# Weight tiles and small tiles move to the upper end of SBUF, streamed operands to the lower end

## The chip, the cores and the metric

The kernel runs on 1 core of a Trainium2 chip. The metric is device time in microseconds (us) of one execution. TensorE (PE) multiplies, ScalarE (ACT) and VectorE (DVE) work element by element, GpSimd (POOL) helps them, SyncE (SP) issues most DMAs. A matmul has two operands in SBUF: a block of 128x128 numbers that a weight load (PEld) puts into the array, and an operand of up to 512 columns that is streamed through it. The load of the next matmul runs while the present one streams.

## The reference

Two transformer-like blocks work on 512 tokens of width 1024, in float32:

```python
x = x + 0.5 * swiglu(rms_norm(x, ffn1_norm), ffn1_w_in, ffn1_w_out)       # hidden width 2816
mix = banded and compressed/selected attention of rms_norm(x) @ w_mix_in
x = x + mix @ w_mix_out
x = x + 0.5 * swiglu(rms_norm(x, ffn2_norm), ffn2_w_in, ffn2_w_out)
proj = rms_norm(x) @ w_in                         # gated linear attention and retention, 4 heads each
h = x + (sigmoid(mga) * (o_gla @ w_br_gla) + sigmoid(mgb) * (o_ret @ w_br_ret)) @ w_out
h = h + experts(rms_norm(h))                      # 32 experts, 2 of 8 in one group for each token
out = rms_norm(h)
```

## The kernel before, in words

Activations lie transposed, a tile for each 128 features with the 512 tokens along its columns. For accuracy every large product is made of three: `split` (L84, L85) makes a rounded high part (float32r) and the rest as a low part, and `mm3` issues high x high (L99), the streamed operand's low part (L100), and the weights' low part (L101). `gemm` runs `mm3` over k-tiles, so a product of 8 k-tiles is 24 matmuls of 128x128 against 128x512.

The stages in order of time: the first FFN (to about 381 us), attention (to about 751), the second FFN (to about 1027), the second mixer with gated linear attention (the pool `gla`) and retention (the pool `ret`; to about 1797), the product with `w_out` and the routing (to about 1860), and the experts (to the end).

`load_w` (L87 on) brings 128x1024 weights from HBM into a tile `wraw` (3 buffers), and splits it into `whi` and `wlo` (2 buffers each). What the matmuls stream:

- `xh`, `xl` (8 tiles each, 2 KB of every partition): the scaled input of a stage. Streamed in the products `pg`, `pu` (FFN in) and `pj` (projections). In `vv` they are the loaded block, and `whi`, `wlo` are streamed. The tiles `oh`, `ol` of the last product of mixer 2 take the same places.
- `hh`, `hl` (10 each): the hidden values of an FFN, streamed in its second product `po`.
- `fh`, `fl` (8 each): the heads' outputs in mixer 2, made in `head_out` (L818), streamed in `ya` and `yb`.
- `rh`, `rl`, `sh`, `sl` and others: attention's inner products. In `rs` both operands are `rh` or `rl`.

SBUF is handed out from two ends. Pools of the lower end are stacked upward in the order in which they are opened, those with `side="right"` downward from the upper end. Before, `const`, `wts`, `xhl` and `small` are opened at the lower end and stay, and the pools of the stages follow above them; only the experts' ring of weights (`ring`, L1087) is at the upper end. The ring is opened in `moe_open` and filled by `fill_ring` while the product with `w_out` runs. A pool that takes the place of a released one waits tile by tile for the last reader of what lay there.

The scheduler keeps the written order on PE, ACT and SP. The expert stage's zeroing of three gather rows `xr` (L1095) is POOL's work behind the adds `mt` (L1060), which end mixer 2.

Of the kernel before, what the change touches and what calls it, by code (L numbers as in the profile page):

```python
# [10 lines left out]
F32R = mybir.dt.float32r  # L11
# [28 lines left out]
class Kern:  # L40
    def __init__(self, ctx, tc, A, out, dbg=None, stop=None):
        self.ctx, self.tc, self.nc, self.A, self.out = ctx, tc, tc.nc, A, out
        self.dbg = dbg or {}
        self.stop = stop
        self.sin = None
        e = ctx.enter_context
        self.const = e(tc.tile_pool(name="const", bufs=1))
        self.wp = e(tc.tile_pool(name="wts", bufs=1))
        self.xp = e(tc.tile_pool(name="xhl", bufs=1))
        self.sm = e(tc.tile_pool(name="small", bufs=2))  # L50
        self.dram = e(tc.tile_pool(name="dram", bufs=1, space=bass.MemoryType.DRAM))
        self.ps = e(tc.tile_pool(name="psum", bufs=1, space=PSUM))
        self.xd = self.dram.tile([128, DT, 512], F32, name="xd")
# [732 lines left out]
    def head_out(self, V, c0, nt, sh, sl, wname, w0, gates, wait):  # L786

        nc = self.nc
        vh, vl = V
        O = []  # L790
        ssum = None
        for t in range(nt):
            po = self.ps.tile([128, 512], F32, name="pvo", tag="tp", bufs=2)
            for j in range(4):
                q = slice(128 * j, 512)
                v = slice(c0 + 128 * t, c0 + 128 * t + 128)
                self.mm3(po[:, q], vh[:, j, v], vl[:, j, v], sh[:, j, q], sl[:, j, q], j == 0, j == 3)
            o = self.m2.tile([128, 512], F32, name="o", bufs=4)
            nc.scalar.activation(o, po, AF.Copy)
            sq = self.m2.tile([128, 512], F32, name="osq", bufs=2)  # L800
            nc.scalar.activation(sq, po, AF.Square)
            if ssum is None:
                ssum = sq
            else:
                nc.gpsimd.tensor_tensor(out=ssum, in0=ssum, in1=sq, op=OP.add)
            O.append(o)
        F = self.F

        def rest():
            p = self.ps.tile([128, 512], F32, name="on", tag="pv", bufs=1)  # L810
            nc.tensor.matmul(p, self.ones, ssum, start=True, stop=True)
            r = self.rstd_from(p, 1.0 / (128 * nt), "hr", None)
            for t in range(nt):
                g = gates[t]
                nc.gpsimd.tensor_tensor(out=g, in0=g, in1=r, op=OP.mult)
                o = O[t]
                nc.vector.scalar_tensor_tensor(o, o, self.vcol(wname, w0 + t), g, op0=OP.mult, op1=OP.mult)
                fh = self.m2.tile([128, 512], F32R, name="fh", bufs=8)  # L818
                fl = self.m2.tile([128, 512], F32R, name="fl", bufs=8)
                self.split(o, fh, fl)  # L820
                F.append((fh, fl))
        self.pend = [wait, rest]
        self.flush(0)
# [165 lines left out]
    def mixer2(self):  # L989
        nc, A = self.nc, self.A  # L990
        self.xpool.release()
        self.m2 = self.pool("m2")
        m3 = self.m3 = self.pool("gla")
        self.gmask = m3.tile([128, 8, 128], I32, name="gmask")
        nc.sync.dma_start(self.gmask, A["gmask"])
        ma = self.dram.tile([128, DT, 512], F32, name="ma")
        yb = self.dram.tile([128, DT, 512], F32, name="yb")
        self.pend = None
        self.gla_decay()
        self.F = []  # L1000
        V = None
        for h in range(4):
            if h == 0:
                V = self.vproj(A["wgv"][:, h // 2], False)
            q, k = self.gla_qk(h)
            gates = [self.silu_tile(A["wg"][:, h, 2 + t]) for t in range(2)]
            if h == 2:
                V = self.vproj(A["wgv"][:, h // 2], False)
            self.gla_core(h, q, k, V, gates)
        for n in range(DT):  # L1010
            _, s = self.sigma(self.proj2(A["wma"][:, n]))
            self.flush()
            w = self.load_w(A["wbg"][:, n])
            po = self.acc("ya")
            self.gemm(po, w, self.F, DT)
            t = self.m2.tile([128, 512], F32, name="mt", tag="gate", bufs=4)
            nc.vector.tensor_tensor(out=t, in0=po, in1=s, op=OP.mult)
            nc.sync.dma_start(ma[:, n], t)
        m3.release()
        m3 = self.m3 = self.pool("ret")  # L1020
        self.cs = m3.tile([128, 2, 512], F32, name="csr")
        nc.sync.dma_start(self.cs, self.csd)
        for c in (0, 1):
            nc.vector.tensor_tensor(out=self.cs[:, c], in0=self.cs[:, c], in1=self.rstd, op=OP.mult)
        M = []
        Q = None
        for half in range(2):
            F = self.F = []
            for h in (2 * half, 2 * half + 1):
                Q = Q or self.ret_qk(h, 0)  # L1030
                K = self.ret_qk(h, 1)
                V = self.vproj(A["wrv"][:, h], True)
                gates = [self.silu_tile(A["wr"][:, h, 4 + t]) for t in range(4)]
                self.ret_core(h, Q, K, V, gates)
                Q = None
            if half == 0:
                Q = self.ret_qk(2, 0)
            if half == 1:
                m3.release()
                sp = self.pool("sig")  # L1040
                sg = []
                for n in range(DT):
                    _, g = self.sigma(self.proj2(A["wmb"][:, n]), sp.tile([128, 512], F32, name=f"sg{n}"))
                    sg.append(g)
            self.flush()
            for n in range(DT):
                w = self.load_w(A["wbr"][:, half, n])
                po = self.acc("yb")
                self.gemm(po, w, self.F, DT)
                t = self.m2.tile([128, 512], F32, name="mt", tag="gate", bufs=4)  # L1050
                if not half:
                    nc.scalar.activation(t, po, AF.Copy)
                    nc.sync.dma_start(yb[:, n], t)
                    continue
                nc.sync.dma_start(t, yb[:, n])
                nc.vector.tensor_tensor(out=t, in0=po, in1=t, op=OP.add)
                nc.vector.tensor_tensor(out=t, in0=t, in1=sg[n], op=OP.mult)
                t2 = self.m2.tile([128, 512], F32, name="mt2", tag="vc", bufs=2)
                nc.sync.dma_start(t2, ma[:, n])
                nc.gpsimd.tensor_tensor(out=t, in0=t, in1=t2, op=OP.add)  # L1060
                h = self.xp.tile([128, 512], F32R, name=f"oh{n}", tag=f"xh{n}")
                lo = self.xp.tile([128, 512], F32R, name=f"ol{n}", tag=f"xl{n}")
                self.split(t, h, lo)
                M.append((h, lo))
        sp.release()
        self.m2.release()
        self.moe_open()
        self.open_x()
        self.route_open()
        for n in range(DT):  # L1070
            w = self.load_w(A["wo2"][:, n])
            r = self.old_x(n)
            if n:
                self.fill_ring(2)
            po = self.acc("po2")
            self.gemm(po, w, M, DT)
            nc.vector.tensor_tensor(out=self.x[n], in0=po, in1=r, op=OP.add)
            if n:
                self.route_tile(n - 1)
        self.route_tile(DT - 1)  # L1080
        self.fill_ring(RING + len(EXTRA) - 2 * (DT - 1))
# [700 lines left out]
```

## Time and profile before

| what | us |
|---|---|
| median of 3 runs | 2369.15 (2362.69 to 2371.07) |
| the profiled execution | 2362.63 |
| its span | 2360.8 |
| PE busy in it | 2285.1 (97%) |
| DVE, ACT, POOL busy | 1151.6, 857.0, 401.6 |
| granted TensorE clock, mean | 0.988 of full speed |

PE's records of successive matmuls overlap: the duration of one (some 0.39 us) is longer than the distance from its start to the next start. What a product costs is read from the distance between starts; the duration helps as a second witness.

### The profile page before, as it was taken

The numbers are of one execution on the slowest core, as the hardware profiler recorded it, in microseconds if no ns is written. First come the engines' busy times: TensorE is split into PE (matmuls) and PEld (weight loads), VectorE is DVE, ScalarE is ACT, GpSimd is POOL, SyncE is SP. The second block draws the span as 40 slices with busy tenths as digits, with TensorE's granted clock in tenths as the row PEclk, the third lists the DMA queues.
The fourth block names the chain that finished last, engine by engine and source line by source line (L and its number), as shares of the span: only waits on it lengthen the run. The fifth ranks groups of instructions, "written<-read, shape, count | busy, mean of one in ns | idle before, by whom it ended". The sixth has DMA issues, their size and how long they took to land.

```text
span 2360.8 us, 27739 instructions
## 1 busy us (share of the span) xinstructions
PE 2285.1 (97%) x10344; PEld 1674.6 (71%) x10344; DVE 1151.6 (49%) x2074; ACT 857.0 (36%) x1441; POOL 401.6 (17%) x408
## 2 busy tenths in 40 slices
PE   8999999999999999999999999999999899999997
PEld 6888888777778888878777887787878544444443
DVE  4534444888754343456684445435464333332223
ACT  4322234677642222354454354434553211100002
POOL 1000002435410000014340112203113201111001
PEclk9999999999999999999999999999999899999999
DMA  4533335221143333332213323232337999999997
GB/s 145 187 91 95 100 96 165 81 72 41 46 121 98 90 93 104 108 115 72 64 53 112 108 84 89 84 117 67 90 116 229 352 394 407 406 407 407 404 408 303
DMA packets 126098, 390.83 MB, mean 166 GB/s; under 512 B 15398, under 2 KB 21071, under 8 KB 125704
## 3 DMA queue, kind: packets, MB, share of 16 engines
q1 hardware_dynamic: 121064, 380.10, 47.1%
q10 hardware_dynamic: 2592, 4.72, 0.5%
q0 software_dynamic: 2304, 4.20, 0.5%
q8 instruction: 83, 1.36, 0.2%
q14 instruction: 55, 0.45, 0.1%
HBM read 378.44 MB, written 17.33 MB: 168 GB/s over the span
## 4 chain that ended last, share of the span: by engine, by line
PE 86%; DVE 5%; DMA 3%; ACT 3%; POOL 1%; issue 1%; SPq 0%; POOLq 0%; DVEq 0%; ACTq 0%
PE pg L1326 5%; PE pj L101 5%; PE pj L100 5%; PE pj L99 5%; PE pu L1326 5%; PE po L100 4%; PE po L101 4%; PE po L99 4%; PE pd L1326 4%; PE pu L101 3%; PE pu L99 3%; PE pu L100 3%; PE pg L99 3%; PE pg L101 3%; PE pg L100 3%; PE py L1393 2%
## 5 line engine op out<-in xcount | busy, mean ns | idle before, releaser
L84 ACT ACTIVATE whi<-wraw 128x1024 fp32r<-128x1024 f32 (+2 forms) x290 | 296.1, 1021 | 714.4 <-issue 185.9
L85 DVE TENSOR_TENSOR wlo<-wraw,whi 128x1024 fp32r<-128x1024 f32 (+2 forms) x282 | 347.4, 1232 | 138.2 <-ACT whi L84 128.5
L101 PE MATMUL pj<-xh,wlo 128*128 128x512 f32 x624 | 247.3, 397 | 10.4 <-DVE wlo L85 10.4
L99 PE MATMUL pj<-xh,whi 128*128 128x512 f32 x624 | 250.2, 401 | 0.0
L100 PE MATMUL pj<-xl,whi 128*128 128x512 f32 x624 | 246.3, 395 | 0.0
L157 POOL TENSOR_TENSOR ssq<-ssq,sq 128x512 f32<-128x512 f32 x34 | 52.6, 1547 | 774.1 <-ACT sq L154 772.1
L1326 PE MATMUL pg<-wexp,xs 128*64 128x512 f32 x474 | 164.4, 608 | 2.4 <-DMA wexp<-in_wexp 2.3
L1326 PE MATMUL pu<-wexp,xs 128*64 128x512 f32 x474 | 160.6, 594 | 0.0
L99 PE MATMUL pg<-xh,whi 128*128 128x512 f32 x352 | 138.6, 394 | 8.7 <-ACT xh L142 7.1
L101 PEld LDWEIGHTS pj<-xh,wlo 128*128 128x128 f32 x624 | 118.4, 190 | 36.0 <-DVE wlo L85 12.1
L100 PE MATMUL po<-hl,whi 128*128 128x512 f32 x352 | 139.6, 397 | 0.0
L99 PE MATMUL po<-hh,whi 128*128 128x512 f32 x352 | 139.5, 396 | 0.0
L101 PE MATMUL po<-hh,wlo 128*128 128x512 f32 x352 | 139.5, 396 | 0.0
L100 PE MATMUL pg<-xl,whi 128*128 128x512 f32 x352 | 138.2, 393 | 0.5 <-DVE xl L143 0.5
L101 PE MATMUL pu<-xh,wlo 128*128 128x512 f32 x352 | 137.2, 390 | 0.9 <-DVE wlo L85 0.9
L101 PE MATMUL pg<-xh,wlo 128*128 128x512 f32 x352 | 137.9, 392 | 0.0
L99 PE MATMUL pu<-xh,whi 128*128 128x512 f32 x352 | 137.1, 389 | 0.0
L100 PE MATMUL pu<-xl,whi 128*128 128x512 f32 x352 | 136.9, 389 | 0.0
L99 PEld LDWEIGHTS pj<-xh,whi 128*128 128x128 f32 x624 | 118.6, 190 | 25.7 <-issue 2.6
L100 PEld LDWEIGHTS pj<-xl,whi 128*128 128x128 f32 x624 | 118.2, 189 | 24.7 <-issue 1.7
L1326 PE MATMUL pd<-wexp,hs 128*64 128x512 f32 x484 | 115.7, 599 | 0.0
L1326 PEld LDWEIGHTS pu<-wexp,xs 128*64 128x64 f32 x474 | 49.1, 138 | 78.4 <-issue 77.9
(613 smaller groups left out, 4418.3 us busy)
## 6 DMA issues: line engine op xcount, KB each, us to landing
wexp<-in_wexp SPq DMA_DIRECT2D x358, 512.0 KB
wraw<-in_w1i SPq DMA_DIRECT2D x44, 512.0 KB
wraw<-in_w2i SPq DMA_DIRECT2D x44, 512.0 KB
wraw<-in_wr SPq DMA_DIRECT2D x32, 512.0 KB
wpark<-in_wexp SPq DMA_DIRECT2D x48, 256.0 KB
wraw<-in_wg SPq DMA_DIRECT2D x16, 512.0 KB
wraw<-in_wrv SPq DMA_DIRECT2D x16, 512.0 KB
wraw<-in_wbr SPq DMA_DIRECT2D x16, 512.0 KB
```

The source lines that it names most:

```text
L84: return (self.nc.scalar.activation(hi, src, AF.Copy), (eng or self.nc.vector).tensor_tensor(out=lo, in0=src, in1=hi.bitcast(F32), op=OP.s ...
L85: (eng or self.nc.vector).tensor_tensor(out=lo, in0=src, in1=hi.bitcast(F32), op=OP.subtract))
L99: mm(ps, ah, bh, start=first, stop=False)
L100: mm(ps, ah, bl, start=False, stop=False)
L101: mm(ps, al, bh, start=False, stop=last)
L157: self.nc.gpsimd.tensor_tensor(out=self.ssq, in0=self.ssq, in1=sq, op=OP.add)
L1326: self.pe(self.nc.tensor.matmul(out[r], x[:, r], self.loaded[2 * p + j, c][half], start=first, stop=last))
L1393: self.pe(nc.tensor.matmul(ps, oh[:, i * 128:i * 128 + 128], y[:, hf * 512:hf * 512 + 512], start=(first and j == 0), stop=(j == 1)))
```

## The change

The pools `wts` (weights) and `small` go to the upper end, so `xhl` follows `const` at the lower end and the stages' pools follow `xhl`. A new pool `m2f`, opened before `m2`, holds `fh` and `fl`.

```diff
         self.const = e(tc.tile_pool(name="const", bufs=1))
-        self.wp = e(tc.tile_pool(name="wts", bufs=1))
         self.xp = e(tc.tile_pool(name="xhl", bufs=1))
-        self.sm = e(tc.tile_pool(name="small", bufs=2))
+        self.wp = e(tc.tile_pool(name="wts", bufs=1, side="right"))
+        self.sm = e(tc.tile_pool(name="small", bufs=2, side="right"))
...
-                fh = self.m2.tile([128, 512], F32R, name="fh", bufs=8)
-                fl = self.m2.tile([128, 512], F32R, name="fl", bufs=8)
+                fh = self.m2f.tile([128, 512], F32R, name="fh", bufs=8)
+                fl = self.m2f.tile([128, 512], F32R, name="fl", bufs=8)
...
         self.xpool.release()
+        self.m2f = self.pool("m2f")
         self.m2 = self.pool("m2")
...
         self.m2.release()
+        self.m2f.release()
         self.moe_open()
```

No instruction is added or removed. Where the tiles lie in the two programs as built, in bytes of a partition (first byte of the first and of the last buffer). Every tile starts at a multiple of 32; "even" means a multiple of 64, "odd" 32 more than one.

| tiles | before | | after | |
|---|---|---|---|---|
| `whi`, `wlo` | 30656 to 42944 | even | 212960 to 225248 | odd |
| `xh`, `xl` (`oh`, `ol`) | 47040 to 77760 | even | 18368 to 49088 | even |
| `hh`, `hl` | 121440 to 160352 | odd | 79808 to 118720 | even |
| `fh`, `fl` | 154208 to 184928 | odd | 51136 to 81856 | even |
| `rh`, `rl` | 203360 to 217696 | odd | 161728 to 176064 | even |
| `sh`, `sl`, `vh`, `vl` | 100960 to 133728 | odd | 92096 to 124864 | even |

In time order one thing moves. Of POOL's queue at the end of mixer 2, before (`mt` are mixer 2's last sums, `xr` the rows for the gather, the rest is routing):

```order
L1060 TENSOR_TENSOR mt<-mt,mt_14108 128x512
L1060 TENSOR_TENSOR mt<-mt,mt_14150 128x512
L1060 TENSOR_TENSOR mt<-mt,mt_14192 128x512
L1095 MEMSET xr_14207 128x1024
L1095 MEMSET xr_14208 128x1024
L1095 MEMSET xr_14209 128x1024
L1170 IOTA io 128x64
L1229 IOTA tok 128x4
L1244 IOTA tokens 128x512
```

The same place of POOL's queue after (the lines are two further down in the changed file):

```order
L1061 TENSOR_TENSOR mt<-mt,mt_14111 128x512
L1061 TENSOR_TENSOR mt<-mt,mt_14153 128x512
L1097 MEMSET xr_14211 128x1024
L1097 MEMSET xr_14212 128x1024
L1061 TENSOR_TENSOR mt<-mt,mt_14195 128x512
L1097 MEMSET xr_14213 128x1024
L1172 IOTA io 128x64
L1246 IOTA tokens 128x512
L1231 IOTA tok 128x4
```

Two of the three MEMSETs now stand ahead of the last `mt` sum, and they wait for the end of the last `yb` product, since the rows now lie where `fh` lay. PE, ACT and SP issue the same instructions in the same order; on DVE one small cast of the routing moves by one place.

## Rows read from the trace of the kernel before

**Rows 1.** The page's first part: busy time of each engine and its share of the span.

```profile
PE 2285.1 (97%) x10344; PEld 1674.6 (71%) x10344; DVE 1151.6 (49%) x2074; ACT 857.0 (36%) x1441; POOL 401.6 (17%) x408
```

**Rows 2.** The page's fourth part: shares of the chain of waits that ended last, by engine.

```profile
PE 86%; DVE 5%; DMA 3%; ACT 3%; POOL 1%; issue 1%; SPq 0%; POOLq 0%; DVEq 0%; ACTq 0%
```

**Rows 3.** Windows by stage: the second FFN, mixer 2, the product with `w_out` and the routing, the experts. Columns: window, its length, then busy time and instructions of PE, PEld, DVE, ACT, POOL, the granted clock, the DMA engines' mean share and GB/s.

```profile
752.00:1027.00 275.00, 275.00 (x1198) 224.73 (x1197) 119.65 (x140) 77.71 (x96) 9.82 (x6) 1.00 0.35 104
1027.00:1802.00 775.00, 752.28 (x3440) 614.77 (x3439) 423.30 (x595) 355.89 (x550) 183.07 (x149) 0.98 0.30 91
1802.00:1860.00 58.00, 55.02 (x316) 46.30 (x315) 24.87 (x54) 22.92 (x37) 11.71 (x12) 1.00 0.92 309
1860.00:2343.00 483.00, 472.57 (x2044) 203.77 (x2046) 141.02 (x359) 50.63 (x97) 56.52 (x80) 0.98 1.02 402
```

**Rows 4.** The experts' weights: the issues of their DMAs on SP's queue, count, duration of an issue in ns, first and last start.

```profile
L1101 SPq DMA_DIRECT2D wexp<-in_wexp x358: 327/328/760, 1801.8 to 2331.5; - x179
```

**Rows 5.** Windows on PE alone that hold one kind of product each: `po` (192 matmuls), `pg` and `pu` (336), `pj` between other work (48), `pj` (96), `vv` (96), `yb` (192). Columns as above, of PE alone; the count takes in a record or two that reach over a window's edge.

```profile
105.88:150.86 44.98, 44.98 (x194) 1.00 0.32 94
150.86:227.03 76.17, 76.17 (x338) 1.00 0.32 93
389.25:400.29 11.04, 11.04 (x50) 1.00 0.67 212
1330.84:1352.61 21.77, 21.77 (x98) 1.00 0.33 94
1352.61:1374.37 21.76, 21.76 (x98) 1.00 0.37 111
1752.30:1797.28 44.98, 44.98 (x194) 1.00 0.48 152
```

**Rows 6.** Lines of the views of the tiles `hh`, `xh` and `rh`: instructions, then duration of one in ns (least, median, most), first and last start, and the shapes.

```profile
L99 PEld LDWEIGHTS po<-hh,whi x352: 187/188/192, 105.7 to 1026.0; 128*128 128x128 f32 x176
L99 PE MATMUL po<-hh,whi x352: 392/397/400, 105.9 to 1026.2; 128*128 128x512 f32 x176
...
L99 PE MATMUL pu<-xh,whi x352: 389/389/497, 16.4 to 986.9; 128*128 128x512 f32 x176
...
L99 PE MATMUL vv<-whi,xh x224: 343/389/754, 400.7 to 1670.1; 128*128 128x512 f32 x96, 128*128 128x408 f32 x16
...
L99 PE MATMUL rs<-rh x32: 221/334/390, 1396.1 to 1696.6; 128*128 128x512 f32 x8, 128*128 128x384 f32 x8, 128*128 128x256 f32 x8, 128*128 128x128 f32 x8
```

**Rows 7.** The timeline of PE where a run of `pj` ends and `rs` follows, four places: start, duration (us), line, operands.

```profile
1395.67 0.39 PE L100 MATMUL pj<-xl,whi 128*128 128x512 f32 x1
1395.90 0.40 PE L101 MATMUL pj<-xh,wlo 128*128 128x512 f32 x1
1396.13 0.39 PE L99 MATMUL rs<-rh 128*128 128x512 f32 x1
...
1397.52 0.33 PE L99 MATMUL rs<-rh 128*128 128x384 f32 x1
...
1480.13 0.40 PE L101 MATMUL pj<-xh,wlo 128*128 128x512 f32 x1
1480.37 0.39 PE L99 MATMUL rs<-rh 128*128 128x512 f32 x1
...
1608.24 0.40 PE L101 MATMUL pj<-xh,wlo 128*128 128x512 f32 x1
1608.47 0.39 PE L99 MATMUL rs<-rh 128*128 128x512 f32 x1
...
1692.31 0.40 PE L101 MATMUL pj<-xh,wlo 128*128 128x512 f32 x1
1692.55 0.39 PE L99 MATMUL rs<-rh 128*128 128x512 f32 x1
```

**Rows 8.** PE's groups by line with shapes kept apart: count | busy us, mean ns of one | idle before. L100 and L101 have as many as L99 in each.

```profile
L99 PE MATMUL pj<-xh,whi 128*128 128x512 f32 x624 | 250.2, 401 | 0.0
...
L99 PE MATMUL pg<-xh,whi 128*128 128x512 f32 x352 | 138.6, 394 | 8.7 <-ACT xh L142 7.1 <-ACT rstd_ln L175 1.6
...
L99 PE MATMUL pu<-xh,whi 128*128 128x512 f32 x352 | 137.1, 389 | 0.0
...
L99 PE MATMUL vv<-whi,xh 128*128 128x512 f32 x192 | 75.5, 393 | 0.0
...
L99 PE MATMUL yb<-fh,whi 128*128 128x512 f32 x128 | 51.3, 401 | 0.4 <-ACT fh L84 0.4
...
L99 PE MATMUL ya<-fh,whi 128*128 128x512 f32 x64 | 26.1, 410 | 1.8 <-ACT fh L84 1.8
...
L99 PE MATMUL po<-oh,whi 128*128 128x512 f32 x64 | 25.4, 397 | 0.0
...
L99 PE MATMUL po<-mh,whi 128*128 128x512 f32 x32 | 13.3, 420 | 1.2 <-ACT mh L84 1.2
...
L99 PE MATMUL pvo<-sh,vh 128*128 128x512 f32 x24 | 9.8, 428 | 0.0
```

**Rows 9.** The timelines of PE and of POOL, and the chain of waits, around the end of mixer 2 (start, duration, what).

```profile
1797.04 0.39 PE L101 MATMUL yb<-fh,wlo 128*128 128x512 f32 x1
...
1801.11 2.74 POOL L1095 MEMSET xr<- 128x1024 f32 x3
...
1799.03 2.16 POOL mt L1060
```

## The prediction

> **What bounds the kernel now.** I read the page's busy times and the shares of its chain first: PE is busy 97% of the span, and 86% of the chain that ended last is PE [rows 1, 2]. The windows by stage say where that holds. In the second FFN PE is busy for all of the 275.0 us, in mixer 2 for 752 of 775 [rows 3]. The experts are another case: there the DMA engines are full (mean share 1.02, 402 GB/s) while PE too looks busy [rows 3], because matmuls wait for weights. Their weights are issued from 1801.8 us on [rows 4], behind the weights of the product with `w_out`, whose buffers PE frees. So the kernel is a PE-bound part of about 1800 us, and a DMA-bound tail that begins when the first part is through. A microsecond that PE loses before 1800 us moves the tail and the end with it; one that it loses in the tail is hidden by the transfers. What the change does to the distance between matmuls before 1800 us is the whole question.
>
> That distance has two values for the same instruction (128 columns loaded, 512 streamed, float32r), both at a granted clock of 1.00 [rows 5]. `pg` and `pu`: 76.17 us / 336 = 226.7 ns. `pj`: 21.77 / 96 = 226.8. `vv`, which loads `xh` and streams `whi`: 21.76 / 96 = 226.7. But `po`, which streams `hh`: 44.98 / 192 = 234.3, and `yb`, which streams `fh`: 234.3. The durations part in the same way, 389 against 397 ns, while a weight load takes 188 ns in either and ends long before the next start, so it is not the load that is waited for [rows 6].
>
> What do the slow ones have in common? By the table of places, `pg`, `pu`, `pj` and `vv` stream and load only tiles at even places within the lowest 80 KB. `po` and `yb` stream from odd places above 120 KB and load `whi` from an even one below 43 KB. Two readings are open: the streamed operand's own place costs the 7.5 ns, or the two operands' places not being alike. One kind of spot tells them apart. Where a run of `pj` ends and `rs` follows, the last `pj` streams `xh` from its good place as always, but the load beside it is already `rs`'s block `rh`, odd and high. In all four places this one matmul takes 0.40 us instead of 0.39, and the next start comes 0.23, 0.24, 0.23 and 0.24 us later, 235 ns on average [rows 7]. The stream was as good as before; only the load's place had changed. I take the second reading: unlike places cost about 7.5 ns a matmul. (Whether "unlike" is the odd 32 bytes or the distance I needn't decide, for after the change the weights are both odd and high.)
>
> **The change part by part.** No engine gets or loses an instruction. Each term is a count [rows 6, 8] (a group of L99 times three) times a difference of distances.
>
> 1. `pg`, `pu`, `pj`: 1,056 + 1,056 + 1,872 = 3,984 matmuls stream `xh`/`xl`, even and low. Their weights go from even and low to odd and high. Distance in a run 226.7 -> 234.2, so 7.5 ns. Not all stand in long runs: between other work 48 `pj` took 11.04 us, 230.0 each [rows 5]. I put 400 of the 3,984 there (an estimate) with 4.2 ns. 3,584 x 7.5 + 400 x 4.2 = 26.9 + 1.7 = +28.6 us.
> 2. `vv`: 576 with 512 columns. They stream the weights, now odd and high, and load `xh`, even and low: 576 x 7.5 = +4.3 us.
> 3. `po` from `hh` (1,056), `ya` (192), `yb` (384) and `po` from `mh` (96): the stream becomes even, the weights odd. One kind of unlike pair takes the place of another: 0. If the streamed operand's place were what counts, this is where the change would gain.
> 4. The product with `w_out` streams `oh`/`ol` from `xh`'s places: 192 x 7.5 = 1.4 us. It lies mostly in the third window, where the ring fills and DMA is at 0.92 [rows 3]: between 0 and 1.4, and I take half, +0.7.
> 5. Mixer 2's inner products (`rs`, `pvo`) have both operands odd before and even after. Six `rs` in sequence take 1397.52 - 1396.13 = 1.39 us, 232 each [rows 7]. Of 512 columns there are 24 `rs` [rows 6] and 72 `pvo` [rows 8]. If they fell to 226.7 that would be 96 x 5 = 0.5 us less, and with the narrower ones at most thrice that, 1.5 (an estimate). They run in short stretches, where even good pairs stand at 230 [rows 5]; I take 0 and keep 1.5 for the range.
> 6. POOL: two MEMSETs now precede the last `mt` sum. They wait for the end of the last `yb` product, which starts at 1797.04 and lasts 0.39, and three take 2.74 us [rows 9], two 1.8 to 1.9. So they end at 1799.2 to 1799.3, and the sum, which began at 1799.03 and is on the chain [rows 9], is held up by 0.2 to 0.4 us; behind it `oh` of the last tile and PE's `po` wait. +0.3.
>
> The moved DVE, ACT and DMA operands I cost at nothing: DVE and ACT have 49% and 36% of the span [rows 1], their work lies beside PE's, and the experts' transfers write the same bytes. If a split of a weight did come late, PE would wait at the `wlo` products, and the page would show it.
>
> Sum: 28.6 + 4.3 + 0.7 + 0.3 = +33.9 us on the profiled execution's 2362.6 (span 2360.8 and 1.8 around it), so 2396.5. That execution was 6.5 us under the median of the three timed runs; on the median the same sum gives 2403. I forecast between the two, 2400.
>
> The price of 7.5 ns for this very pair (even and low streamed, odd and high loaded) was seen only in single matmuls at the end of a run, never in a run of its own. Its bounds: below, 226.7 ns, no cost [rows 5]; above, 236 ns, hardly more than the 235 of the four places [rows 7]: (236 - 234.2) x 4,176 = 7.5 us more, 2404 to 2411. I take 234.2, the nearest row with long runs of unlike places.
>
> **The rivals.**
>
> A. Half the price. `rs` with both operands odd and high runs at 232, between the two values [rows 7]. If the new pairs ran so: 3,584 x 5.0 + 400 x 2 + 4.3 + 0.4 + 0.3 = 23.7 us, 2386 to 2393. For it: `rs` is the only run with loads from such places. Against it: its streams are odd too, and it is short.
>
> B. Only the streamed operand's place counts. Then `po`, `ya`, `yb` and the rest, 1,728 matmuls, fall from 234.2 to 226.7: -13.0 us; `vv` now streams from the bad place: +4.3; POOL +0.3. Net -8.4 us: 2354 to 2361, faster or level. For it: in every long run the stream's place alone sorts fast from slow, and the loads were always from good places, so no run contradicts it. Against it: the four matmuls of [rows 7], slow with an unchanged stream. It decides as soon as `pg` and `pu` keep 226.7.
>
> C. Places don't reach PE in this way, and the 7.5 ns come from something else that goes with the product (its k-tiles, its PSUM user). Then nothing moves but POOL: 2363 to 2369. Against it: `pg`, `pj` and `vv` are different products and agree to 0.1 ns, `po` of the FFN and `yb` of the mixer are different ones and agree as well [rows 5]. [...]
>
> **How the numbers follow.** The forecast's own case, every unlike pair at about 234, gets 0.62, and its own range is 2384 to 2411. Rival A gets 0.12, B 0.13, C 0.08; 0.05 is left for what I don't see, of either sign. The range over all, 2362 to 2411, leaves out B and a little above. About 0.5% (12 us) is what a measurement of this kernel tells from no change: under 2357.3 is faster, over 2381 slower. Faster: half of B and a bit, 0.08. Same: the other half of B, C, and a rest, 0.16. Slower: forecast, A and a rest, 0.76.
>
> **What the profile after would show.** If the forecast holds, windows over `pg`/`pu` in the FFN have 336 matmuls in some 78.7 us instead of 76.17, `pj` and `vv` 96 in 22.5, the medians of `pu` and `vv` go from 389 to 397 ns, and `po` and `yb` stay at 234. The second FFN (275.0 us) takes some 280: twice 336 `pg` and `pu` at 7.5 ns. The DMA-bound window keeps its length and its 402 GB/s and starts some 33 us later. If `po` and `yb` fall to 226.7 while `pg` stays, B is right; if `pg` and `pu` rise to 230 to 232, A. The prediction is wrong from the start if idle time of PE appears that waits for ACT or DVE, or if the experts' window changes its length.

## The result

The changed kernel takes 2389.44 us (median of 4 runs, 2386.93 to 2390.12) against 2366.96 for the kernel before (4 runs, 2362.69 to 2371.07): slower, with a ratio of 1.0094 (95% interval 1.0079 to 1.0108). The forecast was 2400, between 2362 and 2411. The profiled executions stand further apart than the medians, 2389.55 against 2362.63, since the one of before was among its fastest; the traces are compared over these 26.9 us.

The page of the kernel after, its first part and the shares of its chain, which answer to [rows 1, 2]:

```profile
PE 2314.8 (97%) x10344; PEld 1678.0 (70%) x10344; DVE 1151.3 (48%) x2074; ACT 857.9 (36%) x1441; POOL 402.4 (17%) x408
...
PE 87%; DVE 5%; ACT 3%; DMA 3%; POOL 1%; issue 1%; POOLq 0%; SPq 0%; DVEq 0%; ACTq 0%
```

PE is busy for 29.7 us more with the same 10,344 matmuls; DVE, ACT and POOL are as busy as before to a microsecond. No work was added: each matmul takes longer. The windows on PE alone that answer to [rows 5] (`po`, then `pg`/`pu`, `pj`, `vv`, `yb`; columns: window, length, PE busy and count, granted clock, DMA share, GB/s):

```profile
108.89:153.69 44.80, 44.80 (x194) 1.00 0.33 94
153.69:232.09 78.40, 78.40 (x338) 1.00 0.32 91
1347.81:1370.21 22.40, 22.40 (x97) 1.00 0.34 97
1370.21:1392.61 22.40, 22.40 (x97) 1.00 0.34 104
1778.80:1823.60 44.80, 44.80 (x194) 1.00 0.47 152
```

Where there were two distances there is one: 44.80 / 192 = 78.40 / 336 = 22.40 / 96 = 233.3 ns. `pg`, `pu`, `pj` and `vv` take 6.6 ns more a matmul, `po` and `yb` 0.9 less (before, 234.2 or 234.3). The second FFN, from the start of its first `po` run to the end of its last, shows both; first the window of before, then that of after:

```profile
750.92:1026.93 276.01, 276.01 (x1201) 225.56 (x1200) 120.43 (x141) 78.72 (x95) 9.82 (x6) 1.00 0.35 104
```

```profile
760.17:1040.17 280.00, 280.00 (x1201) 225.45 (x1200) 120.48 (x141) 78.74 (x95) 9.81 (x6) 1.00 0.35 102
```

672 `pg` and `pu` at 6.6 ns are 4.4 us, 528 `po` at -0.9 are -0.5: 3.9 of the 4.0 us. PE is busy through the whole of both windows, so no wait has any part in it.

The experts' weights, after, against [rows 4]:

```profile
L1103 SPq DMA_DIRECT2D wexp<-in_wexp x358: 327/328/757, 1828.2 to 2358.4; - x179
```

The first issue comes 26.4 us later than before, and from the first to the last it is 530.2 us against 529.7. The DMA-bound tail was moved, not stretched: in the 400 us from 100 us behind the first issue the DMA engines are at 1.03 of full with 406 GB/s in both kernels (before from 1901.80 us, after from 1928.20).

### The profile page after: what moved, and what is told of

It reads as the page before. It is cut to its first block, busy times and chain, and to the rows that moved or that the text cites. A ratio compares the mean times of both kernels' runs of the same rounds, so it can differ in the third digit from the quotient of the medians.

```text
span 2387.7 us, 27732 instructions
## 1 busy us (share of the span) xinstructions
PE 2314.8 (97%) x10344; PEld 1678.0 (70%) x10344; DVE 1151.3 (48%) x2074; ACT 857.9 (36%) x1441; POOL 402.4 (17%) x408
## 3 DMA queue, kind: packets, MB, share of 16 engines
q8 instruction: 83, 1.36, 0.2%
## 4 chain that ended last, share of the span: by engine, by line
PE 87%; DVE 5%; ACT 3%; DMA 3%; POOL 1%; issue 1%; POOLq 0%; SPq 0%; DVEq 0%; ACTq 0%
PE pg L1328 5%; PE pj L101 5%; PE pj L99 5%; PE pj L100 5%; PE pu L1328 5%; PE po L100 4%; PE po L99 4%; PE po L101 4%; PE pd L1328 4%; PE pg L99 3%; PE pg L100 3%; PE pg L101 3%; PE pu L99 3%; PE pu L101 3%; PE pu L100 3%; PE py L1395 2%
## 5 line engine op out<-in xcount | busy, mean ns | idle before, releaser
L101 PE MATMUL pj<-xh,wlo 128*128 128x512 f32 x624 | 251.1, 403 | 9.5 <-DVE wlo L85 9.5
L99 PE MATMUL pj<-xh,whi 128*128 128x512 f32 x624 | 254.5, 408 | 0.0
L100 PE MATMUL pj<-xl,whi 128*128 128x512 f32 x624 | 250.0, 401 | 0.0
L99 PE MATMUL pg<-xh,whi 128*128 128x512 f32 x352 | 141.3, 401 | 8.5 <-ACT xh L142 7.0
L101 PEld LDWEIGHTS pj<-xh,wlo 128*128 128x128 f32 x624 | 118.8, 190 | 38.6 <-DVE wlo L85 11.3
L100 PE MATMUL pg<-xl,whi 128*128 128x512 f32 x352 | 140.9, 400 | 0.5 <-DVE xl L143 0.5
L101 PE MATMUL pg<-xh,wlo 128*128 128x512 f32 x352 | 140.5, 399 | 0.0
L101 PE MATMUL pu<-xh,wlo 128*128 128x512 f32 x352 | 139.4, 396 | 0.8 <-DVE wlo L85 0.8
L99 PEld LDWEIGHTS pj<-xh,whi 128*128 128x128 f32 x624 | 119.3, 191 | 28.6 <-issue 2.2
L99 PE MATMUL pu<-xh,whi 128*128 128x512 f32 x352 | 139.3, 396 | 0.0
L100 PE MATMUL po<-hl,whi 128*128 128x512 f32 x352 | 139.3, 396 | 0.0
L100 PE MATMUL pu<-xl,whi 128*128 128x512 f32 x352 | 139.2, 396 | 0.0
L99 PE MATMUL po<-hh,whi 128*128 128x512 f32 x352 | 139.2, 396 | 0.0
L101 PE MATMUL po<-hh,wlo 128*128 128x512 f32 x352 | 139.2, 395 | 0.0
L100 PEld LDWEIGHTS pj<-xl,whi 128*128 128x128 f32 x624 | 119.0, 191 | 27.9 <-issue 1.7
```

The costliest lines, as they stand in the source:

```text
L99: mm(ps, ah, bh, start=first, stop=False)
L100: mm(ps, ah, bl, start=False, stop=False)
L101: mm(ps, al, bh, start=False, stop=last)
```

## Experiments

After the result the question was what makes a pair of operands "unlike". Theory 1: an odd multiple of 32 bytes in one of the two starts. Theory 2: the distance between the two places, or loads from the upper end. All twelve kernels change places only: eleven by small unused tiles (a pad of 8 float32 columns is 32 bytes of each partition), e4 by leaving out `m2f`. The places given are those of the programs as built. They are told apart by the distance between matmuls in the same windows as above; times are given beside it.

**e1, the changed kernel with its weights 32 bytes lower.**

```diff
+        self.pad = e(tc.tile_pool(name="pad", bufs=1, side="right")).tile([128, 8], F32, name="padt")
         self.wp = e(tc.tile_pool(name="wts", bufs=1, side="right"))
```

> The changed kernel with a pad of 32 bytes above the weights at the upper end, so that weights, x's parts and the streamed operands all start at multiples of 64 (even), as far apart as in the changed kernel. Theory 1 (a streamed and a loaded operand that differ in the odd 32 bytes cost): pg, pu, pj and vv fall from 233.3 to 226.7 ns, po, ya and yb too. About 4,000 x 6.6 = 26 us, vv 3.5, 1,728 x 6.6 = 11 us: some 40 us less than the changed kernel, about 2350. Theory 2 (the distance between the two, or loads from the upper end, cost): all stay at 233.3 and the time at about 2389.

2355.96 us, ratio to before 0.9955 (0.9940 to 0.9971). The windows of `po`, `pg`/`pu`, `vv`, `yb`:

```profile
108.05:151.56 43.51, 43.51 (x193) 1.00 0.32 97
151.56:227.72 76.16, 76.16 (x337) 1.00 0.30 94
1344.47:1366.23 21.76, 21.76 (x97) 1.00 0.33 110
1745.02:1788.54 43.52, 43.52 (x193) 1.00 0.49 156
```

All at 226.7 ns, `po` and `yb` for the first time. The pools are where the change put them, some 190 KB apart for `xh`, and the streamed operands haven't moved at all; moving the weights by 32 bytes took 33 us off. Theory 2 is out.

**e2, the kernel before with its stages 32 bytes higher**, so that `hh`, `fh`, `rh` and the stages' other tiles start at multiples of 64.

```diff
         self.sm = e(tc.tile_pool(name="small", bufs=2))
+        self.pad = e(tc.tile_pool(name="pad", bufs=1)).tile([128, 8], F32, name="padt")
```

> The kernel before with a pad of 32 bytes behind small, so that the stages' operands (hh, fh, rh and others) become even while everything stays where it was but for 32 bytes; the weights and x were even already. Theory 1: po, ya, yb and po from mh fall from 234.2 to 226.7, 1,728 x 7.5 = 13 us: about 2354. Theory 2: hh and fh are as far from the weights as before, nothing moves: about 2367.

2363.32 us, ratio 0.9990 (0.9980 to 0.9999). `po` and `pg`/`pu`:

```profile
109.11:153.91 44.80, 44.80 (x194) 1.00 0.30 95
153.91:230.09 76.18, 76.18 (x338) 1.00 0.30 93
```

`po` goes from 234.2 to 233.3, not to 226.7. So theory 1 is wrong as well: multiples of 64 on both sides are not enough. (The forecast's 1,728 holds 96 matmuls of `po` from `mh` too many: `mh` lies at the upper end, above the pad's reach. The right count is 1,632, here and in e12.)

**e3, the kernel before with only the weights at an odd multiple of 32**: a 32-byte pad ahead of `wts`, another behind it.

> The kernel before with 32 bytes ahead of the weights and 32 behind them: weights odd, x's parts even, hh and fh odd as they were, all within 64 bytes of their places. Theory 1 in its form 'unlike pairs cost': pg, pu, pj, vv go to 233.3 (+26 and +3.5 us), po, ya, yb are odd with odd and fall to 226.7 (-13): about 2384. Theory 1 in its form 'each odd operand costs': pg as before said, but po goes up to about 240 (+10): about 2406. Theory 2: nothing moves, about 2367.

2387.02 us, ratio 1.0079 (1.0057 to 1.0101). `po` and `pg`/`pu`:

```profile
109.17:153.96 44.79, 44.79 (x193) 1.00 0.30 95
153.96:232.35 78.39, 78.39 (x337) 1.00 0.29 91
```

The time fits the first forecast and its reason doesn't: `pg` is at 233.3 as expected, but `po`, odd with odd, is there too, neither at 226.7 nor at 240. So the slow distance can be had at the lower end, with the weights 32 bytes from where they were.

**e4, the changed kernel without `m2f`** (`fh` and `fl` in `m2` again).

> The changed kernel without the pool m2f: fh and fl lie in m2 as before, still even, some 60 KB higher. POOL's two MEMSETs go back behind the last mt sum. If 32 bytes are what counts, ya and yb stay at 233.3 and the time at the changed kernel's 2389, less the 0.2 to 0.4 us by which the last mt sum is held up, which only the trace can show (from the last yb product to the sum's start). If the place low in SBUF has a worth of its own, ya and yb (576 matmuls) go back to 234.2 or more, +0.5 us.

2386.45 us, ratio 1.0089 (1.0069 to 1.0109), the changed kernel's within the intervals. `yb` stays at 44.80 us for 192. What the pool did to POOL's order has to be read from the trace: after, then e4 (POOL's timeline; each kernel's last `yb` matmul is the row of PE above it).

```profile
1823.37 0.40 PE L101 MATMUL yb<-fh,wlo 128*128 128x512 f32 x1
...
1823.83 1.85 POOL L1097 MEMSET xr<- 128x1024 f32 x2 [1.92 <-PE yb L101]
1825.64 1.86 POOL L1061 TENSOR_TENSOR mt<-mt,mt 128x512 f32<-128x512 f32 x1
...
1828.94 0.50 PE L100 MATMUL po<-ol,whi 128*128 128x512 f32 x1
```

```profile
1817.50 0.40 PE L101 MATMUL yb<-fh,wlo 128*128 128x512 f32 x1
...
1819.48 2.15 POOL L1060 TENSOR_TENSOR mt<-mt,mt 128x512 f32<-128x512 f32 x1 [3.45 <-ACT whi L84]
...
1823.08 0.50 PE L100 MATMUL po<-ol,whi 128*128 128x512 f32 x1
```

Behind the MEMSETs the sum starts 2.27 us after the last `yb`, without them 1.98: held up by 0.29. But it then takes 1.86 us instead of 2.15, and ends 4.13 us after the start of that `yb` in both; why it is shorter isn't shown. The `po` that waits for it starts 5.57 us after that `yb`, against 5.58.

With both theories gone I listed the starts modulo larger numbers, that is, what is left of the first byte when multiples of the number are taken off (47040 is 183 x 256 + 192, so `xh` of before is at 192 modulo 256). In e1 and in the fast pairs of before, weights and streams are alike modulo 256 (both at 192). In e2 `po` streams from 128 and loads from 192, in e3 from 160 and 224. The next four kernels ask for the period; they are the changed kernel with a pad above the weights of 160, 288 or 96 bytes, and one with a pad of 96 there and 64 ahead of `xhl`.

**e5 and e6.**

> As the run of the changed kernel with a 32-byte pad, but the weights lie another 128 bytes lower: 160 bytes of pad. Weights and streams are alike modulo 128 (both 64), but no longer modulo 256. Theory 1b (the two starts have to be alike modulo 128): pg and po stay at 226.7, about 2356. Rival (the period is 256 or 512 bytes): 233.3 in both, about 2389 like the changed kernel.

> 288 bytes of pad: weights and streams are alike modulo 256, not modulo 512. Theory 1b: 226.7 in pg and po, about 2356. Period of 256: 226.7 as well, while the run with 160 bytes is slow. Period of 512 (the step from one k-tile's block of weights to the next): 233.3, about 2389.

e5: 2384.24 us (ratio 1.0070, 1.0053 to 1.0087). e6: 2354.79 (0.9946, 0.9930 to 0.9963). `po` and `pg`/`pu`, first e5, then e6:

```profile
110.03:154.64 44.61, 44.61 (x194) 1.00 0.33 95
154.64:232.72 78.08, 78.08 (x338) 1.00 0.32 91
```

```profile
109.34:152.87 43.53, 43.53 (x194) 1.00 0.34 97
152.87:229.02 76.15, 76.15 (x337) 1.00 0.32 94
```

Alike modulo 128 alone gives 232.3 to 232.4 ns (e5), alike modulo 256 but not 512 gives 226.7 (e6). In these runs the period is 256 bytes: theory 1b (alike modulo 128) gives way to theory 1c (alike modulo 256).

**e7**, which I had meant as a test of 128.

> Weights, x's parts and the streamed operands all start at multiples of 128: a pad of 64 bytes ahead of x's parts, one of 96 above the weights. If being alike modulo 128 is what counts (theory 1b): 226.7 in pg and po, about 2356. Rival: only a start at 64 beyond a multiple of 128 is fast, as all fast operands so far had it: 233.3 in pg and po, about 2389.

2381.77 us (ratio 1.0060, 1.0043 to 1.0077); `po` 44.61 us for 192, `pg`/`pu` 78.08 for 336. Its weights are at 128 and its streams at 0 modulo 256, so it is the pair of e5 once more and says nothing on its rival, which e9 and e10 take up.

**e8.**

> 96 bytes of pad: weights at multiples of 128, streams 64 beyond one. Both are even (multiples of 64), as in the run of the kernel before with its stages made even, with the two swapped. Theory 1b: pg and po at 233.3, about 2389. If only the weights' own place has to be a multiple of 64 (the second run's 233.3 then being due to the stage's place): 226.7, about 2356.

2370.60 us (ratio 1.0006, 0.9995 to 1.0018), a miss for both. `po`, and three neighbours in mixer 2, `pj`, `vv`, `pj`:

```profile
108.02:151.97 43.95, 43.95 (x193) 1.00 0.33 96
...
1332.32:1354.29 21.97, 21.97 (x97) 1.00 0.32 93
1354.29:1376.69 22.40, 22.40 (x97) 1.00 0.36 109
1376.69:1399.09 22.40, 22.40 (x97) 1.00 0.32 94
```

`po` has 228.9 ns, between the two known values; of two runs of `pj` with the same places one has 228.9 and one 233.3. `vv`, where stream and load have changed sides, has 233.3. So the price depends on the offset with its sign, and at this offset it has two states.

**e9 and e10, alike at other places**: pads of 224 above the weights and 64 ahead of `xhl` (all starts at 0 modulo 256), and of 192 and 96 (all at 32).

> Weights, x's parts and the streamed operands all at multiples of 256 (pads of 64 bytes ahead of x's parts, 224 above the weights). The eight runs so far have 226.7 ns wherever stream and load start alike modulo 256, but in each of these both were 192 beyond a multiple of 256. Theory 1c (alike modulo 256): 226.7 in pg, po and vv, about 2356. Rival (the two must be at 192): 232 to 234, about 2385.

> All at 32 beyond a multiple of 256, so that both operands are odd multiples of 32 (pads of 96 and 192 bytes). Theory 1c: 226.7 in pg, po and vv, about 2356: an odd multiple of 32 costs nothing where both have it. Rival (an odd multiple of 32 costs by itself, as in the reading that each odd operand costs): 233 or more, 2385 or more.

e9: 2348.22 us (ratio 0.9922, 0.9907 to 0.9937). e10: 2352.94 (0.9944, 0.9929 to 0.9960). `po` and `pg`/`pu`, first e9, then e10:

```profile
108.59:152.11 43.52, 43.52 (x193) 1.00 0.33 97
152.11:228.27 76.16, 76.16 (x337) 1.00 0.33 94
```

```profile
106.53:150.06 43.53, 43.53 (x194) 1.00 0.33 97
150.06:226.21 76.15, 76.15 (x337) 1.00 0.33 94
```

226.7 in both, as in e1 and e6 with weights and streams at 192. In these kernels the place itself costs nothing, not even an odd multiple of 32 (e10); what counts is the offset, the streamed operand's start less the loaded one's.

**e11**, the changed kernel with a pad of 128 above the weights.

> Pad of 128: the weights at 96, the streams at 192 beyond a multiple of 256, so the stream is 96 ahead of the load in pg, pj and po, and 96 behind in vv. Theory 1c with a price that is the same for all unlike pairs: 232 to 234 in all, about 2385. Rival (the price depends on the offset, since the run with the stream 64 ahead had 228.9 in pg and po): another value in pg than in vv, where 234.2 is known from the kernel before (96 behind); I can't say which value.

2388.29 us (ratio 1.0086, 1.0070 to 1.0102). `pg`/`pu`, then `vv`:

```profile
155.23:233.63 78.40, 78.40 (x338) 1.00 0.31 91
1369.42:1391.89 22.47, 22.47 (x97) 1.00 0.35 103
```

`pg`/`pu` have 78.40 / 336 = 233.3 ns; `vv` has 22.47 / 96 = 234.1, which `po` of before has, too, at the same offset (234.2). The two sides of an offset differ here too, by 0.8 ns.

**e12, the kernel before with 96 bytes behind `small`**, every pool at its old end.

```diff
         self.sm = e(tc.tile_pool(name="small", bufs=2))
+        self.pad = e(tc.tile_pool(name="pad", bufs=1)).tile([128, 24], F32, name="padt")
```

> The kernel before with 96 bytes of pad behind small and nothing else: the stages' operands go from 96 to 192 beyond a multiple of 256, where weights and x's parts are already; all pools stay at the ends where they were. Theory 1c: po, ya, yb at 226.7, 1,728 x 7.5 = 13 us: about 2355, as fast as the changed kernel with its weights made alike, so the ends of SBUF have no worth of their own. Rival (the lower place is worth something besides): between 2356 and 2367.

2353.58 us (ratio 0.9942, 0.9928 to 0.9955). `po`, `pg`/`pu`, `yb`:

```profile
106.44:149.96 43.52, 43.52 (x193) 1.00 0.33 97
149.96:226.12 76.16, 76.16 (x337) 1.00 0.32 94
...
1745.58:1789.10 43.52, 43.52 (x194) 1.00 0.50 156
```

One line added to the old layout gives what e1, e6 and e10 give in the new one. The ends of SBUF have no worth of their own. (The size is less sure than the distances: 14.6 us between the medians, 10.7 to 17 by the interval, but 7.7 between the spans of the two profiled executions, 2360.8 and 2353.1, where 1,632 x 7.5 would be 12.2.)

One product is a witness for which no kernel was made: `po` from `mh`, attention's last product. `mh` lies at the upper end (the experts' ring is not alone there), so this `po` is at offset 32 before, at 96 after, and at 0 only in e3, where the FFN's `pg` and `po` are slow. Windows on it of before, after and e3, with 83, 88 and 80 distances:

```profile
642.28:661.65 19.37, 19.37 (x85) 1.00 0.43 123
...
647.91:668.44 20.53, 20.53 (x89) 1.00 0.40 116
...
650.85:669.03 18.18, 18.18 (x82) 1.00 0.44 131
```

They are 233.4, 233.3 and 227.3 ns: the one alike pair is the fast one here too.

All kernels together, by the offset of the streamed operand's start from the loaded one's, modulo 256 bytes; every distance was measured in the runs named, at a granted clock of 1.00:

| offset | where | ns between starts |
|---|---|---|
| 0 | before `pg` `pu` `pj` `vv`; these and `po` `yb` in e1, e6, e9, e10, e12; e3 `po` from `mh` | 226.7, 227.3 |
| 32 | after `vv`; e3 `pg`; before `po` from `mh` | 233.3, 233.4 |
| 64 | e8 `pg` `po` | 228.9, some runs 233.3 |
| 96 | e11 `pg` `po`; after `po` from `mh` | 233.3 |
| 128 | e5, e7 | 232.3 to 233.2 |
| 160 | before `po` `yb`; e11 `vv` | 234.1 to 234.3 |
| 192 | e2 `po`; e3 `po`; e8 `vv` | 233.3 |
| 224 | after `pg` `pj` `po` `yb`; e4 | 233.3 |

Two products or more stand at the same offset in every row, most of them from tiles at different places, with nearly the same distance. What in the hardware has a period of 256 bytes was not tried and stays open.

## Why the prediction was right

The direction, the mechanism and the range were right, and the size was a quarter too large: +33.9 us by the sum, 26.9 between the profiled executions. The time alone doesn't tell the forecast's own case (2384 to 2411) from rival A (2386 to 2393), since 2389.44 lies in both; the windows do, with 233.3 ns where the forecast had 234.2 and A 231.7.

- *What bounds.* PE's loss before 1800 us went to the end one for one: the experts' first issue came 26.4 us later, the span grew by 26.9.
- *Which reading.* Unlike places cost, and not the streamed operand's place: `pg` streams from the lowest place it ever had and went from 226.7 to 233.3, and e1, which moves the weights alone, brings it back. The four matmuls of [rows 7] were the right witness; their stream at 192 and load at 96 have offset 96, which e11 measured in long runs at 233.3. In e12 the same stream meets `rh` at 192, and the slow step is gone at all four spots (0.39 us, and 0.22 or 0.23 to the next start), of which one is:

```profile
1388.39 0.39 PE L102 MATMUL pj<-xh,wlo 128*128 128x512 f32 x1
1388.61 0.39 PE L100 MATMUL rs<-rh 128*128 128x512 f32 x1
```

  To leave open what "unlike" is was sound: weights at an odd multiple of 32 and streams at an even one can only have the offsets 32, 96, 160 and 224, and all four cost 6.6 to 7.6 ns. For an even offset it would have been luck (0: nothing, 64: 2.2).
- *The load.* That a load "ends long before the next start" is too much: by the trace of before, in the windows of [rows 5], it lasts 188 ns and ends 36 ns ahead of the next start in `pg` and `pu`, 44 in `po`. That the load isn't longer where the distance is 234.3 holds; the difference lies between its end and that start.
- *Term 1, mis-sized.* "7.5 ns", taken from the long runs of `po` and `yb`, was the price of offset 160, the dearest of the eight. The new pairs have offset 224 and 6.6 ns: 3,584 x 6.6 = 23.7 us instead of 26.9. In mixed stretches the 4.2 were too few: the 48 `pj` that took 11.04 us take 11.30 after, 5.4 each:

```profile
396.40:407.70 11.30, 11.30 (x49) 1.00 0.66 205
```

- *Term 2* likewise: `vv` at 233.3, 576 x 6.6 = 3.8 instead of 4.3.
- *Term 3, wrong at 0.* "One kind of unlike pair takes the place of another" is true, but the kinds differ: `po` from `hh`, `ya` and `yb` gain 0.9 ns x 1,632 = 1.5 us. The 96 of `po` from `mh`, which the prediction counted at 234.2, were at 233.4 and stay at 233.3.
- *Term 4, +0.7, right in size.* The product with `w_out` takes 0.8 us longer from its first to its last start (before, then after), of which at most 0.5 shows in the tail (530.2 us against 529.7):

```profile
1797.28:1848.19 50.91, 50.74 (x264) 1.00 0.87 287
...
1823.60:1875.32 51.72, 51.67 (x264) 1.00 0.85 282
```

- *Term 5, 0,* held: six `rs` take 1.39 us after as before.
- *Term 6, wrong at +0.3.* The last sum was held up by 0.29 us as computed, and gave it back by taking 1.86 instead of 2.15 us; e4 has the same end without the MEMSETs.

So the first three terms come to 23.7 + 400 x 5.4 + 3.8 - 1.5 = 28.1 us, 1.7 more than the 26.4 by which the experts' first issue is later. Most of what is left over is the 400: more of `pj` stands among other work than that. Over all starts in the two traces that lie under 250 ns apart, `pg` and `pu` take 6.5 ns more, `pj` 5.6 and `vv` 6.5, the 1,632 take 0.9 less: 13.8 + 10.5 + 3.7 - 1.5 = 26.5 us. (The waits in between aren't in this sum and differ by a microsecond or so, so the last digit is luck.)

Rival A rested on `rs` at 232. Both operands of `rs` were at 96 modulo 256, an alike pair, so it said nothing on unlike ones. (The sum of A also charges `vv` 7.5 ns; at A's own 5.0 it is 22.3 us instead of 23.7.) That its runs of six were at 232 is no price of their own places: `rh` lies at the same bytes after and in e1, and `rs` takes 1.39 us for six after, behind `pj` at 233.3 ns, but 1.36 in e1, behind `pj` at 226.7, which is 226.7 each for `rs` too. (Before, the one unlike step of [rows 7] stood right ahead of them.) After, then e1:

```profile
1415.01 0.39 PE L99 MATMUL rs<-rh 128*128 128x512 f32 x1
...
1416.40 0.33 PE L99 MATMUL rs<-rh 128*128 128x384 f32 x1
```

```profile
1387.99 0.39 PE L100 MATMUL rs<-rh 128*128 128x512 f32 x1
...
1389.35 0.33 PE L100 MATMUL rs<-rh 128*128 128x384 f32 x1
```

Rival B is refuted by `pg` and e1, rival C by e12: 96 bytes of padding alone take `po` and `yb` from 234.2 or 234.3 ns to 226.7, and `pg` and `pu` stay at 226.7. C had 2363 to 2369 us for this change, and the profiled execution took 2389.55: at a granted clock of 1.00 the distance goes from 226.7 (before, `pg`) to 234.3 ns (before, `po`) by the offset of PE's own two operands.

The forecast was laid between the profiled execution and the median of before. After's median lies on its profiled execution, before's 4 us above its own, so the medians show 22.5 us where the traces show 26.9.

## What to carry to other kernels

In a long run of float32r matmuls, where the next 128x128 block is loaded while the present operand streams, read the distance between starts by product before looking for waits: two values for one shape at a granted clock of 1.00 (226.7 and 234.3 ns before) pointed to places here. Then work out the tiles' starts modulo 256 bytes, the period in these runs (e5, alike modulo 128 alone: 232.3 ns; e6, alike modulo 256 but not 512: 226.7), and pad by a few columns until streamed and loaded operands agree; here one line is worth 14.6 us by the medians (e12, 2353.58 beside 2368.17) where moving whole pools cost 22. Look also at what an unrelated pool's odd size (`small`, 12,960 bytes) does to all that is stacked behind it.

## What was not expected

- e9 is the fastest of all, 2348.22 us beside 2368.17 for the kernel before in the same session, and some 5 us under e10 and e12, which have the same distances on PE. The difference is in the experts' tail. The windows of 400 us from 100 us behind the first issue, first e9, then e12 (last column GB/s):

```profile
1891.40:2291.40 400.00, 398.42 (x1750) 172.71 (x1748) 122.66 (x303) 42.85 (x84) 45.31 (x65) 1.00 1.03 412
```

```profile
1893.70:2293.70 400.00, 398.10 (x1726) 170.95 (x1723) 117.86 (x295) 41.52 (x81) 44.77 (x64) 1.00 1.03 406
```

  The DMA engines are as full, and move 412 GB/s instead of 406. From the first to the last issue e9 takes 523.4 us and e12 530.0; all thirteen others lie between 527.6 and 531.0. The rate goes with the number of the experts' weight tiles, 408 in all, that start at a multiple of 256: 125 in e9, 48 in e3 and e7, none in the eleven other programs. Those eleven have 406 GB/s in this window, e3 and e7 408:

```profile
1928.40:2328.40 400.00, 397.27 (x1732) 170.25 (x1728) 117.83 (x295) 42.18 (x82) 44.76 (x64) 1.00 1.03 408
...
1923.10:2323.10 400.00, 397.35 (x1731) 170.90 (x1728) 118.83 (x297) 42.17 (x82) 44.75 (x64) 1.00 1.03 408
```

  No kernel moves these tiles alone, so that their places are the cause isn't shown.
- At an offset of 64 a product has two states, 228.9 and 233.3 ns, for whole runs of 96 matmuls (e8). All three runs of `pj` at 233.3 (they start at 1376.69, 1462.12 and 1591.47 us) stand directly behind a run of `vv`, which has 233.3 itself; two others behind `vv` (1061.49 and 1676.99 us) have 229.0. What chooses between the two stays open.
